# Conditioning weights fetched a step ahead into tiles of their own in the first layer of a three-block kernel

## The chip, the cores and the metric

The kernel runs on one core of one Trainium2 chip. The metric is the device time of one execution, in microseconds (us). One execution was also recorded by the hardware profiler; its rows are what the argument below is made from.

## What is computed

The input `x` is 1024 positions by 1024 channels in float32. Three blocks follow each other: a gated recurrent block (layer 0), a gated delta-rule block (layer 1) and a hybrid block of convolution and state space. Only layer 0 is touched by the change. Cut to what matters:

```python
c_act = silu(c)                                   # 1024 numbers
for i in range(2):
    cond = c_act @ ada_w[i] + ada_b[i]            # ada_w[i]: 1024 x 3072
    shift, scale, gate = cond[:1024], cond[1024:2048], cond[2048:]
    h = rmsnorm(x, norm_g[i]) * (1 + scale) + shift
    x = x + gate * block_i(h)

def block_0(h):                                   # rglru_block
    xb, zg = split(h @ in_w)                      # 1024 + 1024 columns
    xf = causal_dwconv(xb, conv_w) + conv_b       # 4 taps
    r, i = sigmoid(xf x gate_w[0..1] + gate_b)    # 8 blocks of 128 x 128
    a = exp(-8 * r * softplus(-lam))
    hseq = scan(a, sqrt(1 - a * a) * i * xf)      # along positions
    return (hseq * silu(zg)) @ out_w
```

`cond` has six parts, three for each layer: part 0 is the shift, 1 the scale, 2 the gate. Layer 0 needs its parts 1 and 0 before and during its input projection and its part 2 in its output projection. Parts 1 and 0 of layer 1 are needed by the norm that follows that output projection, part 2 of layer 1 only at the end of layer 1.

## The kernel before, in words

Channels lie on the 128 partitions and positions along the free dimension. A float32 matrix product is made as three float16 products of a high and a low half (`mm_chT`, L108 to L113; `mm_t`, L115 to L120). A weight set of 256 columns (`load_w`, L99) is fetched as one load of 1 MB into a staging tile `wst` (tag `st`, a ring of two), ScalarE makes the high half (L104), VectorE the low half (L105); that frees the staging tile. `wh` and `wl` are rings of four.

**Front (up to about 73 us).** `x` is loaded, normed and transposed in two halves of 512 positions. `ada_load` (L355) makes part 1 of layer 0, then part 0: for each it loads four blocks `sta` of 1 MB, sums 32 products on VectorE (`ada_acc`, L146 to L150, tile `accs`), turns the sums into columns by transposes on TensorE (L135) and a reduce (L368). `put_hT` (L376) writes the scaled halves `hTh` and `hTl`, and `lru_proj` (L297) projects the first pair of blocks. In the traced order part 0 (L410) stands ahead of the second half's `put_hT` (L414) and of its projection (L417).

**Recurrent stage (about 73 to 298 us).** Channels are taken as four pairs of blocks. `xbranch(p)` (L450) projects, convolves (`lru_conv`, L309), makes the gates (L482 to L485), and ends in the scan (L503) that writes `hs`. The gate tiles `gt0`, `gt1` have one buffer, so the gates of a pair wait for the scan of the pair before. `zbranch(p)` (L506) projects the other half, applies SiLU into `zs` (L515, a ring of three), multiplies by `hs` (L516) and writes high and low halves into a tile `y` (L517 through `split`, L122 to L125). `hs` and `y` share a ring of five (tag `a4`). Projections go through three banks `psmm`.

Between the branches stand nine calls of `ada_step` (L522). Each finishes the part taken up a step earlier (`ada_fin`, L162: four transposes, a reduce, an addition and a store) and takes up the next (`ada_part`, L152): two loads of 1 MB into the same `wst` ring that the weights use, followed at once by one multiplication (L148) and seven multiply-adds (L150) of 128x512 on VectorE. Eight half parts are made this way.

**Output projection (about 298 to 385 us).** For each of eight blocks of 128 positions, `out_proj` (L268) multiplies `y` by four weight sets, applies the gate (L276), adds `x` (L277), stores the result, and `norm_to_hT` (L242) makes the input of layer 1.

**What sets the order.** Engines run their instructions strictly in order. The framework fixes that order when the program is built: the order of the source is the priority, work under `tc.high_priority()` goes ahead, and what is ready by its own estimate of time is placed. All loads and stores of this part are issued by one queue, SyncE's (SP), also in order: an issue that waits for a tile holds those behind it.

## Time and profile before

| | us |
|---|---|
| median of 3 runs | 1914.98 |
| lowest, highest | 1912.77, 1927.49 |
| span of the profiled execution | 1914.6 |

The profile gives busy times of the engines: PE (TensorE matmuls), PEld (its weight loads, which overlap), DVE (VectorE), ACT (ScalarE), POOL (GpSimd), SP (SyncE). "PEclk" is the clock granted to TensorE as a share of full speed. A row of the timeline names start, duration, engine, line, operation, tiles and count; in brackets is how long the engine sat idle before it and what ended that. A wait is put down to the releaser that came last.

### The profile page before, as it was taken

The numbers are of one execution on the slowest core, as the hardware profiler recorded it, in microseconds if no ns is written. First come the engines' busy times: TensorE is split into PE (matmuls) and PEld (weight loads), VectorE is DVE, ScalarE is ACT, GpSimd is POOL, SyncE is SP. The second block draws the span as 40 slices with busy tenths as digits, with TensorE's granted clock in tenths as the row PEclk, the third lists the DMA queues.
The fourth block names the chain that finished last, engine by engine and source line by source line (L and its number), as shares of the span: only waits on it lengthen the run. The fifth ranks groups of instructions, "written<-read, shape, count | busy, mean of one in ns | idle before, by whom it ended". The sixth has DMA issues, their size and how long they took to land.

```text
span 1914.6 us, 29618 instructions
## 1 busy us (share of the span) xinstructions
PE 1808.0 (94%) x11847; PEld 1133.6 (59%) x11847; DVE 1450.2 (76%) x2472; ACT 935.7 (49%) x1673; POOL 52.8 (3%) x130
## 2 busy tenths in 40 slices
PE   5799789999899999999999999899999999999998
PEld 3344338855466656687878859556444444444487
DVE  6898876655786678877637689999999999594333
ACT  6567563356555666666434443465463121482221
POOL 0000001000000000001000020000000000000000
PEclk8899899999988899999889999999999999999999
DMA  9343255313131131224324322111221112102212
GB/s 336 108 154 85 93 154 188 105 52 84 31 88 39 27 102 30 79 78 138 91 93 155 115 37 71 38 51 53 92 75 54 57 56 77 45 23 66 78 67 89
DMA packets 161635, 165.26 MB, mean 86 GB/s; under 512 B 45662, under 2 KB 139934, under 8 KB 161498
## 3 DMA queue, kind: packets, MB, share of 16 engines
q1 hardware_dynamic: 161498, 163.38, 27.5%
q8 instruction: 93, 1.52, 0.3%
q14 instruction: 44, 0.36, 0.1%
HBM read 139.05 MB, written 23.12 MB: 85 GB/s over the span
## 4 chain that ended last, share of the span: by engine, by line
PE 51%; DVE 29%; ACT 7%; DMA 6%; issue 6%; SPq 1%; POOL 0%; DVEq 0%; ACTq 0%; POOLq 0%
DVE cc L990 5%; PE psmm L112 3%; PE psmm L111 3%; PE psmm L113 3%; DVE wl L105 2%; DMA wst_ada<-in_ada_w_dram 2%; PE ps_out L120 2%; PE ps_out L118 2%; PE ps_out L119 2%; DVE Tt L763 2%; DVE tm L761 2%; PE ps_fin L118 1%; PE ps_fin L120 1%; PE ps_fin L119 1%; PE ps_zc L113 1%
## 5 line engine op out<-in xcount | busy, mean ns | idle before, releaser
L111 PE MATMUL psmm<-hTh,wh 128*128 128x512 f16 x896 | 347.3, 389 | 19.9 <-ACT zs L515 16.7
L112 PE MATMUL psmm<-hTl,wh 128*128 128x512 f16 x896 | 347.6, 388 | 0.1
L113 PE MATMUL psmm<-hTh,wl 128*128 128x512 f16 x896 | 346.4, 387 | 0.0
L990 DVE SCALAR_TENSOR_TENSOR cc<-cu,cols,cc 128x1024 f32<-128x1024 f32 (+1 forms) x270 | 302.2, 1170 | 0.9
L112 PEld LDWEIGHTS <-wh 128*128 128x128 f16 x1568 | 155.0, 99 | 194.7 <-issue 29.5
L113 PEld LDWEIGHTS <-wl 128*128 128x128 f16 x1568 | 155.1, 99 | 179.3 <-issue 13.4
L111 PEld LDWEIGHTS <-wh 128*128 128x128 f16 x1568 | 155.1, 99 | 178.0 <-issue 12.0
L105 DVE SCALAR_TENSOR_TENSOR wl<-wst,wh 128x2048 f16<-128x2048 f32 (+2 forms) x71 | 154.3, 2177 | 57.8 <-ACT wh L104 57.6
L104 ACT ACTIVATE wh<-wst 128x2048 f16<-128x2048 f32 (+2 forms) x71 | 128.6, 1813 | 116.8 <-PE ps_gs L112 27.7
L763 DVE TENSOR_TENSOR Tt<-Tt,tm 128x248 f32<-128x248 f32 (+30 forms) x248 | 77.7, 313 | 4.5
L761 DVE TENSOR_TENSOR tm<-Lp,Tt 128x248 f32<-128x248 f32 (+30 forms) x248 | 76.9, 310 | 4.2
L118 PE MATMUL ps_z<-wh,hTh 128*128 128x256 f16 x256 | 72.1, 282 | 0.0
L119 PE MATMUL ps_z<-wh,hTl 128*128 128x256 f16 x256 | 72.0, 281 | 0.0
L120 PE MATMUL ps_z<-wl,hTh 128*128 128x256 f16 x256 | 71.9, 281 | 0.0
L120 PE MATMUL ps_out<-wl,y 128*128 128x256 f16 x256 | 69.8, 273 | 0.1
L118 PE MATMUL ps_fin<-wh,merged 128*128 128x256 f16 x256 | 69.8, 273 | 0.0
L119 PE MATMUL ps_fin<-wh,merged 128*128 128x256 f16 x256 | 69.8, 273 | 0.0
L120 PE MATMUL ps_fin<-wl,merged 128*128 128x256 f16 x256 | 69.8, 273 | 0.0
L118 PE MATMUL ps_out<-wh,y 128*128 128x256 f16 x256 | 69.7, 273 | 0.0
L119 PE MATMUL ps_out<-wh,y 128*128 128x256 f16 x256 | 69.7, 273 | 0.0
L123 ACT ACTIVATE hTh<-ps_ht 128x512 f16<-128x512 f32 x32 | 17.3, 594 | 83.2 <-PE ps_ht L252 83.2
L701 ACT ACTIVATE jk<-ps_tk 128x128 f32<-128x128 f32 x128 | 35.7, 279 | 39.7 <-PE ps_tk L697 36.7
(535 smaller groups left out, 4171.7 us busy)
## 6 DMA issues: line engine op xcount, KB each, us to landing
wst<-in_w_in_dram SPq DMA_DIRECT2D x24, 1024.0 KB
wst_ada<-in_ada_w_dram SPq DMA_DIRECT2D x16, 1024.0 KB
wst<-in_gdn_in_w_dram SPq DMA_DIRECT2D x16, 1024.0 KB
xt<-in_x_dram SPq DMA_DIRECT2D x16, 512.0 KB
wst<-in_lru_in_w_dram SPq DMA_DIRECT2D x8, 1024.0 KB
sta<-in_ada_w_dram SPq DMA_DIRECT2D x8, 1024.0 KB
x_d<-xt SPq DMA_DIRECT2D x16, 512.0 KB
wst<-in_lru_out_w_dram SPq DMA_DIRECT2D x4, 1024.0 KB
```

Of the source, the lines that this page charges most:

```text
L104: act.activation(hi, st, AF.Copy, scale=WS)
L105: dve.scalar_tensor_tensor(out=lo, in0=st, scalar=WS, in1=hi, op0=ALU.mult, op1=ALU.subtract)
L111: pe.matmul(ps, wh[:, k, c0:c0 + P], ah(k), start=(k == 0), stop=False)
L112: pe.matmul(ps, wh[:, k, c0:c0 + P], al(k), start=False, stop=False)
L113: pe.matmul(ps, wl[:, k, c0:c0 + P], ah(k), start=False, stop=(k == nk - 1))
L118: pe.matmul(ps, ah(k), wh[:, k, :], start=(k == 0), stop=False)
L119: pe.matmul(ps, al(k), wh[:, k, :], start=False, stop=False)
L120: pe.matmul(ps, ah(k), wl[:, k, :], start=False, stop=(k == nk - 1))
L701: act.activation(jk, pst[:, P * c:P * (c + 1)], AF.Square, accum_out=kq[:, n, 4 * b + c:4 * b + c + 1])
L761: dve.tensor_tensor(out=tv, in0=Lp[:, j, j + 1:].unsqueeze(1).to_broadcast([P, 8, n]), in1=Tt[:, :, j:j + 1].to_broadcast([P, 8, n]), op=A ...
L763: dve.tensor_tensor(out=Tt[:, :, j + 1:], in0=Tt[:, :, j + 1:], in1=tv, op=ALU.subtract)
L990: dve.scalar_tensor_tensor(out=acc, in0=cus[j][:, i + t0:i + t0 + n], scalar=col("cw", j, i), in1=acc, op0=ALU.mult, op1=ALU.add)
```

## The change

1. `ada_part` is split into `ada_fetch` and `ada_sum`. A half part is fetched into four tiles `ast` of 128x1024 (512 KB each, a ring of four of its own) by four loads. The first fetch stands ahead of the recurrent stage; each `ada_step` now finishes an older half part, sums the one fetched a step before, and fetches the next. The sum tile `ad` has one buffer instead of two.
2. Part 2 of layer 1 (two of the eight half parts) leaves the recurrent stage. It is made with the old `ada_part` inside the output projection, after its blocks 3 and 5 in the source, and finished after the loop. The stage keeps six half parts and seven `ada_step`s.
3. The four transposes of `ada_fin` get high priority.
4. `zbranch` writes its high and low halves over the part of `hs` that it has just multiplied; the `a4` ring goes from five to four. The `zs` ring goes from three to two.
5. `xp` (input of the convolution) is a ring of three for all pairs, where odd and even pairs had two each.
6. In the front the second half's `put_hT`, its projection and the column parameters are traced ahead of part 0, and the load of the weight set `wz[0]` behind it.

Everything else in the file differs by removed comments only. The instructions of the arithmetic are the same in number and shape.

```diff
+    def ada_fetch(pl, l, part, h):
+        tiles = []
+        for kk in range(4):
+            st = pl.tile([P, 2, 512], F32, tag="ast", name="ast", bufs=4)
+            sp.dma_start(st, ada_src(l, part, h, 2 * kk, 2))
+            tiles.append(st)
+        return tiles, l, part, h
+
+    def ada_sum(pl, tiles, l, part, h):
+        acc = pl.tile([P, 512], F32, tag="ad", name="ad")
+        for kk, st in enumerate(tiles):
+            for k in range(2):
+                ada_acc(acc, st[:, k, :], 2 * kk + k)
+        return acc, l, part, h
...
     def ada_fin(pl, acc, l, part, h):
-            pe.transpose(pst[:, P * kk:P * (kk + 1)], acc[:, P * kk:P * (kk + 1)], ident)
+            pe_ht(pst[:, P * kk:P * (kk + 1)], acc[:, P * kk:P * (kk + 1)], ident)
...
-        xp = (pl if p % 2 else gwp).tile([P, T + 3], F32, tag="xp", name="xp", bufs=2)
+        xp = gwp.tile([P, T + 3], F32, tag="xp", name="xp", bufs=3)
...
         load_x(1)
+        prows = load_cols(pl, PB, 7)
         wx.append(load_w(a["lru_in_w"][0], WC))
         norm_x(1)
-        wz.append(load_w(a["lru_in_w"][0], D))
+        for k in range(NK):
+            put_hT(xTp(1, k), k, 1)
+        for e in range(2):
+            lru_proj(xps[e], wx[0], e, 1)
+        with tc.high_priority():
+            set_cols(*prows)
         ada_load(0)
...
-        for k in range(NK):
-            put_hT(xTp(1, k), k, 1)
-        prows = load_cols(pl, PB, 7)
-        for e in range(2):
-            lru_proj(xps[e], wx[0], e, 1)
-        with tc.high_priority():
-            set_cols(*prows)
+        wz.append(load_w(a["lru_in_w"][0], D))
...
-                hs = ypool.tile(PR, F32, tag="a4", name="hs", bufs=5)
+                hs = ypool.tile(PR, F32, tag="a4", name="hs", bufs=4)
...
-                y = ypool.tile([P, 2, 2, T], F16, tag="a4", name="y", bufs=5)
...
-                        zs = pl.tile([P, 512], F32, tag="zs", name="zs", bufs=3)
+                        zs = pl.tile([P, 512], F32, tag="zs", name="zs", bufs=2)
...
-                        split(y[:, e, 0, HF[hf]], y[:, e, 1, HF[hf]], zs)
-            adq = [(l, part, h) for l, part in ((0, 2), (1, 1), (1, 0), (1, 2)) for h in range(2)]
-            adp = []
+                        y = hseq[p][:, e, HF[hf]].bitcast(F16)
+                        yT[-1].append((y[:, :512], y[:, 512:]))
+                        split(y[:, :512], y[:, 512:], zs)
+            adq = [(l, part, h) for l, part in ((0, 2), (1, 1), (1, 0)) for h in range(2)]
+            adt, adp = [ada_fetch(pl, *adq.pop(0))], []
...
                 if adp:
                     ada_fin(pl, *adp.pop(0))
+                if adt:
+                    adp.append(ada_sum(pl, *adt.pop(0)))
                 if adq:
-                    adp.append(ada_part(pl, *adq.pop(0)))
+                    adt.append(ada_fetch(pl, *adq.pop(0)))
...
                 if i > 0:
                     norm_to_hT(pl, i - 1, xo.pop(i - 1), G, SH)
+                if i in (3, 5):
+                    adp.append(ada_part(pl, 1, 2, len(adp)))
+            for q in adp:
+                ada_fin(pl, *q)
```

## Rows read from the trace of the kernel before

**Rows 1.** The page: span, busy time of two engines, and 40 slices of PE

```profile
span 1914.6 us, 29618 instructions
PE 1808.0 (94%) x11847; PEld 1133.6 (59%) x11847; DVE 1450.2 (76%) x2472; ACT 935.7 (49%) x1673; POOL 52.8 (3%) x130
...
PE   5799789999899999999999999899999999999998
```

**Rows 2.** Busy time by stretch: stretch, length, each engine's busy us, clock, DMA, GB/s

```profile
46.00:62.00 16.00, 7.00 (x38) 4.70 (x37) 15.80 (x37) 7.60 (x12) 0.00 (x0) 0.70 0.28 73
62.00:73.00 11.00, 11.00 (x57) 5.21 (x56) 6.19 (x20) 3.33 (x7) 0.14 (x2) 0.98 0.00 0
...
73.00:298.00 225.00, 195.56 (x1133) 94.80 (x1131) 185.87 (x224) 147.90 (x161) 5.51 (x9) 0.94 0.45 134
...
298.00:368.00 70.00, 70.00 (x644) 63.23 (x642) 46.66 (x79) 16.54 (x31) 1.54 (x2) 1.00 0.41 129
```

**Rows 3.** Chain of waits through 73 to 298 us: shares, then pieces (start, us, what)

```profile
by line: DMA wst_ada<-in_ada_w_dram 20.4%; DVE ad L150 11.1%; DMA wst<-in_lru_out_w_dram 6.5%; DVE xf L312 6.5%; DVE hs L503 5.9%; DMA wst<-in_lru_in_w_dram 5.0%; DVE wl L105 3.9%; ACT wh L104 3.4%; issue 3.2%; DVE gt L496 2.0%; DVE at L500
...
115.81 8.30 DMA wst_ada<-in_ada_w_dram
...
203.35 11.30 DMA wst_ada<-in_ada_w_dram
...
257.74 14.67 DMA wst<-in_lru_out_w_dram
```

**Rows 4.** The instructions on `wst_ada`: ns min/median/max, first and last start; idle until

```profile
L150 DVE SCALAR_TENSOR_TENSOR ad<-wst_ada,ccol,ad x56: 701/752/755, 92.7 to 257.0; 128x512 f32<-128x512 f32 x56
...
L148 DVE TENSOR_SCALAR ad<-wst_ada,ccol x8: 478/484/488, 90.8 to 247.1; 128x512 f32<-128x512 f32 x8
...
  DMA wst_ada<-in_ada_w_dram: 14.4, 5
```

**Rows 5.** Timeline of VectorE: the longest of the five waits, and the scan behind it

```profile
214.68 0.75 DVE L150 SCALAR_TENSOR_TENSOR ad<-wst_ada,ccol,ad 128x512 f32<-128x512 f32 x1 [5.60 <-DMA wst_ada<-in_ada_w_dram]
215.35 4.46 DVE L503 TENSOR_TENSOR_SCAN hs<-gt,at 128x1024 f32<-128x1024 f32 x2
```

**Rows 6.** PE's waits, 38 to 300 us: in total, times, longest

```profile
PE psmm L111 <- ACT zs L515: 16.7, 5, 7.4
PE ps_ada L135 <- DVE accs L150: 8.3, 3, 7.0
PE ps_ada L166 <- DVE ad L150: 5.4, 1, 5.4
```

**Rows 7.** The instructions on `ps_ada`: ns min/median/max, first and last start

```profile
L167 DVE TENSOR_REDUCE adac<-ps_ada x8: 682/686/692, 108.6 to 259.5; 128x4 f32<-128x512 f32 x8
...
L166 PE MATMUL ps_ada<-ident,ad x32: 272/273/448, 104.1 to 259.1; 128*128 128x128 f32 x32
```

**Rows 8.** Timeline of ScalarE: its longest wait for a weight load in the stage

```profile
272.43 1.91 ACT L104 ACTIVATE wh<-wst 128x2048 f16<-128x2048 f32 x1 [7.24 <-DMA wst<-in_lru_out_w_dram]
```

**Rows 9.** Timeline of TensorE: its longest wait in the stage

```profile
277.95 0.58 PE L111 MATMUL psmm<-hTh,wh 128*128 128x512 f16 x1 [7.38 <-ACT zs L515]
```

**Rows 10.** Timeline of VectorE in the front: sums of part 0

```profile
52.36 4.04 DVE L150 SCALAR_TENSOR_TENSOR accs<-sta,ccol,accs 128x256 f32<-128x256 f32 x10
```

**Rows 11.** Timeline of TensorE in the front: its longest wait there

```profile
56.15 0.66 PE L135 MATMUL ps_ada<-ident,accs 128*128 128x128 f32 x2 [6.99 <-DVE accs L150]
```

**Rows 12.** Chain of waits, 38 to 73 us: single matmuls of 128x512 at both clocks

```profile
62.07 0.43 PE psmm L112
...
64.08 0.22 PE psmm L111
```

**Rows 13.** Lines, 73 to 298 us: the convolution's multiply-adds; busy us, mean ns, idle before

```profile
L312 DVE SCALAR_TENSOR_TENSOR xf<-xp,cols,xf 128x1024 f32<-128x1024 f32 x24 | 30.7, 1282 | 0.8 <-ACT xf L310 0.6
```

**Rows 14.** Waits of SP's queue, 72 to 300 us: in total, times, longest

```profile
SPq L157 <- DVE ad L150: 39.3, 10, 12.5
...
SPq L101 <- DVE ad L150: 15.3, 4, 7.3
```

**Rows 15.** ScalarE's wait for input weights, 72 to 300 us: in total, times, longest

```profile
ACT wh L104 <- DMA wst<-in_lru_in_w_dram: 13.0, 4, 4.4
```

More of the change, by code (lines that the diff above doesn't have):

```diff
@@ L150, in ada_acc, with ada_src @@
             dve.scalar_tensor_tensor(out=acc, in0=st, scalar=ccol[:, k:k + 1], in1=acc, op0=ALU.mult, op1=ALU.add)
+    def ada_src(l, part, h, k0, n):
+        c0 = D * part + 512 * h
+        return a["ada_w"][l, P * k0:P * (k0 + n), c0:c0 + 512].rearrange("(k p) c -> p k c", p=P)
+    def ada_fetch(pl, l, part, h):
[11 more added lines that the diff above has]
+        return acc, l, part, h
     def ada_part(pl, l, part, h):
@@ L155, in ada_part @@
             st = wstage("wst_ada").rearrange("p (k c) -> p k c", k=4)
-            c0 = D * part + 512 * h
-            sp.dma_start(st, a["ada_w"][l, 4 * P * kk:4 * P * (kk + 1), c0:c0 + 512].rearrange("(k p) c -> p k c", p=P))
+            sp.dma_start(st, ada_src(l, part, h, 4 * kk, 4))
             for k in range(4):
@@ L506, in zbranch @@
             def zbranch(p, w):
-                y = ypool.tile([P, 2, 2, T], F16, tag="a4", name="y", bufs=5)
                 sb = shift_proj(w)
                 for e in range(2):
-                    yT.append(y[:, e])
+                    yT.append([])
                     for hf in range(2):
@@ L540 @@
             zbranch(1, wz[1])
-            ada_step()
             wz.append(load_w(a["lru_in_w"][0], D + 3 * WC))
@@ L544 @@
             xbranch(3, wx[3])
-            ada_step()
             ada_step()
@@ L559 @@
                 if i < NT:
-                    xo[i] = out_proj(ws, lambda k, i: yT[k][:, 0, P * i:P * (i + 1)],
-                                     lambda k, i: yT[k][:, 1, P * i:P * (i + 1)], pl, GA, i, x_in[TS[i], :])
+                    xo[i] = out_proj(ws, lambda k, i: yT[k][i // 4][0][:, TS[i % 4]],
+                                     lambda k, i: yT[k][i // 4][1][:, TS[i % 4]], pl, GA, i, x_in[TS[i], :])
                     sp.dma_start(x1_d[TS[i], :], xo[i])
```

## The prediction

> **What bounds the kernel now.** The page comes first: TensorE is busy for 94% of the span, and its lowest digits after the start lie in slices 2 and 4 to 7 of 40, which are layer 0 [rows 1]. The busy times by stretch then show three states of layer 0 [rows 2]. From 46 to 62 us VectorE is the limit (15.8 of 16 us) and TensorE works 7.0 us; in the next 11 us it is the other way round (VectorE 6.2, TensorE 11.0). From 73 to 298 us, the recurrent stage, none is full: TensorE 195.6 of 225, VectorE 185.9, ScalarE 147.9. From 298 to 368 us TensorE is full and VectorE two thirds busy.
>
> So the recurrent stage has room, and the chain of waits shows what holds it: loads of the conditioning weights are its largest item, 20.4% of 225 us, their sums the second with 11.1%, the loads of the output weights the third with 6.5% [rows 3]. That is not 46 us to be won. A load on the chain may have been issued late because something else was late, and with it gone the next slowest chain counts. The tile's own rows say what the engine lost: five waits of VectorE, 14.4 us in all [rows 4]. The longest, 5.6 us, stands directly before the scan of the third pair [rows 5], and the next pair's gates wait for that scan, so it moves everything behind it. TensorE's waits are the other side of the same stage: 16.7 us for `zs`, 5.4 us for a conditioning sum, inside the 225 - 195.6 = 29.4 us that it stood idle [rows 2, 6].
>
> **The change part by part.** The sum goes against the profiled execution, 1914.6 us; the median of the runs is 0.4 us higher, so I take a result of the sum for the median.
>
> *Fetch a step ahead.* A half part's load is issued one `ada_step` earlier, into tiles that the weights do not share. The stage has eight branches in 225 us, 28 us each. The two longest conditioning loads on the chain took 8.3 and 11.3 us [rows 3]. A load issued a branch ahead should have landed: the 14.4 us of waits go. Bounds: 0 (the wait moves to another operand) to 14.4.
>
> *The two half parts moved.* One costs VectorE 0.484 + 7 x 0.752 = 5.75 us [rows 4], a reduce of 0.69 us [rows 7], and an addition I leave out: 6.4 us, 12.9 for both. VectorE was busy for 185.9 of the 225 - 14.4 = 210.6 us in which no such wait held it, but the recurrence also passes through ScalarE and TensorE; I count about half, 6 us. Bounds 0 to 12.9.
>
> *The ring of staging tiles.* The first load of output weights started at 257.7 us, when the last sums (to 257.0 + 0.7) had freed a staging tile, and took 14.7 us [rows 3, 4]. ScalarE stood 7.24 us at the conversion behind it [rows 8], and the halves of `y` stood behind that, so `zs` stayed full and TensorE waited 7.38 us at 277.95 [rows 9]. After the change no conditioning sum holds a staging tile in this stage: 7.4 us, bounds 0 to 7.4.
>
> Together 14.4 + 6 + 7.4 = 27.8 us. These overlap: a scan that comes earlier meets the next limit. I take 0.7 of it, 19.5 us, because three engines that are each 65 to 87% busy do not give back all of a wait; bounds 0 and the removal of TensorE's whole idle time, 29.4 us, with part of what its low clock cost. The granted clock of the stage was 0.94 [rows 2]; with two levels of 1 and one half that is 12% of 225 = 27 us at the low one, half of it lost: 13.5 us.
>
> *Front.* VectorE worked off the ten multiply-adds of part 0 at 52.4 us [rows 10] while TensorE waited 7.0 us [rows 11] and the halves `hTl` were outstanding. With these first, the projection starts earlier and the sums run under it. VectorE remains the limit of the front, so its idle time in 62 to 73 us, 11.0 - 6.2 = 4.8 us, is the bound. I take 4; bounds 0 and 9 (TensorE's idle time in 46 to 62 us).
>
> *`zs` with two tiles.* One half product less can wait for its scan. A half is 24 matmuls of 0.22 us [rows 12], 5.2 us. Where the last scan is late, TensorE stops one half sooner and has that half left over: +5.2 us once. Bounds: 0 (the halves of `y` now come without the load in their way) to 15.6, three of four branches.
>
> *Part 2 of layer 1 in the output projection.* Eight transposes at 0.27 us, 2.2 us by their durations; they are pipelined and I count 1.2 us on TensorE, which is full there; bounds 0 and 2.2. The 12.9 us of VectorE lie under TensorE: 46.7 + 12.9 = 59.6 of 70 us [rows 2]. If that cover were gone, a load of 8 to 11 us would hold VectorE and, past the three banks, TensorE.
>
> *The rest at nothing.* `xp` with three tiles: hidden as long as three multiply-adds of 1.28 us [rows 13] end before the block after next is projected; at worst one such chain, 3.8 us, for three pairs, 11.5 us. `hs` written over: each half is read by the multiplication just before, so the only new waits are VectorE's and ScalarE's own order. The first fetch: TensorE's and VectorE's work of the front hides it, the DMA being idle from 62 to 73 us [rows 2].
>
> Sum: 1914.6 - 4 - 19.5 + 5.2 + 1.2 = 1897.5, which I give as 1897 us.
>
> **What the queue could do to it.** SP issues in order. Conditioning loads already waited there 39.3 us for sums, and weight loads 15.3 us for the same sums [rows 14]. After the change four fetches stand in that queue instead of two, each waiting for the sums of the half part before, and weight loads behind them wait too. ScalarE already stood 13.0 us, four times, for input weights [rows 15]. On this the Trainium skill, "DMA: Bandwidth & Descriptors", section "Anatomy of one DMA — SWDGE (gpsimd) path", says that any semaphore wait happens on the issuing sequencer before dispatch; by that rule, the rows agreeing, a blocked fetch delays every later load on SP.
>
> **The rivals.**
>
> *A. TensorE becomes the limit.* The waits were the whole of the recurrence's excess: TensorE's idle time falls from 29.4 to 5 us, 8 of the 13.5 us of low clock return, the front gives 4, the transposes take 1.2: 1914.6 - 24.4 - 8 - 4 + 1.2 = 1879 us. For it: the waits stand before the scans. Against: `zs` is shorter, and ScalarE is busy for 148 us with an order of its own.
>
> *B. The waits are replaced.* VectorE meets the next operand, `zs` costs its half once, and of the 27.8 us only about a third, 9.7, arrives, with 2 in the front: 1914.6 - 9.7 - 2 + 5.2 + 1.2 = 1909 us. For it: the sums themselves remain on the chain for six of eight half parts.
>
> *C. Weights late in SP's queue.* Each of five input weight loads waits for one more half part's sums, 5.75 us, in front of ScalarE: +29 us on the forecast, 1926 us; this decides once a load is late by over 3.5 us on average (17/5). Against: before, the shared ring made the same loads wait for the same sums.
>
> *D. A fetch does not fit into its step.* If a 512 KB load took as long as one of 1 MB and the four ran one after another, a half part would take 4 x 8.3 = 33 us, 5 more than the 28 us of a branch; six of them cost 30 us, and the 14.4 us would not be saved (0.7 x 14.4 = 10): 1897 + 30 + 10 = 1937 us. It decides from 7 us a load. Against: the DMA share in the stage is 0.45 [rows 2], and loads overlap. The Trainium skill, same page, section "Bandwidth", speaks for this side: it asks for loads of at least 1 MiB to reach 75% of peak, and the change halves them. By that section loads get less efficient; how much at this size no run here shows.
>
> **How the numbers follow.** Chances: the forecast (1888 to 1904) 0.44, A 0.20, B 0.25, C 0.07, D 0.04. A measurement of this kernel tells about 1% from no change, 19 us: below 1895.5 or above 1934. Faster by that: A and half of the forecast, 0.42; slower: D and little of C, 0.05; within 1%: 0.53. The range reaches from A's bound to above B and leaves out C and D and the best of A: 1874 to 1918.
>
> **What would show it.** Right: VectorE's idle time before L148 and L150 near zero in the stage; TensorE's wait for `zs` well under 16.7 us, with nothing like 7.4 us before the output projection; the stage's length, from the gates' weights to the first `ps_out`, near 205 us; TensorE full through the output projection. Wrong: ScalarE waiting for `wst` for more than 22 us in the stage (C); VectorE waiting for `ast` (D); TensorE's wait for `zs` as long as before (B); waits in the output projection behind `wst_ada`.

## The result and the profile after

The changed kernel takes 1930.2 us (median of 20 runs, 1924.1 to 1933.3) beside 1918.5 us for the kernel before (20 runs): a ratio of 1.0058 with the interval 1.0045 to 1.0071. So it is some 11 us slower, where 1897 us was forecast; 1930 lies above the range of 1874 to 1918, and the difference is under the 1% that the prediction called no change. The profiled execution of after spans 1926.9 us, that of before 1914.6 [rows 1].

The page of after, its span, busy times and the 40 slices of TensorE:

```profile
span 1926.9 us, 29657 instructions
...
PE 1814.7 (94%) x11847; PEld 1137.5 (59%) x11847; DVE 1447.6 (75%) x2472; ACT 937.0 (49%) x1674; POOL 51.2 (3%) x130
...
PE   5786998999899999999999999899999999999998
```

Against [rows 1] slice 4 falls from 9 to 6, slices 5 and 6 rise, slices 3 and 7 lose one, and the rest is the same. In before the low digits of layer 0 are those of slices 5 and 6 (7 and 8); the prediction's "slices 2 and 4 to 7" counts 4 and 7, which are 9, with them. The busy times by stretch say more (stretch, length, busy us of PE, PEld, DVE, ACT and POOL with their instructions, granted clock, DMA share, GB/s):

```profile
46.00:62.00 16.00, 15.91 (x90) 8.62 (x89) 8.52 (x11) 10.35 (x16) 0.00 (x0) 1.00 0.33 111
62.00:73.00 11.00, 10.36 (x50) 4.72 (x49) 11.00 (x29) 4.18 (x4) 0.00 (x0) 1.00 0.17 49
73.00:298.00 225.00, 188.16 (x1092) 91.50 (x1091) 180.78 (x227) 147.05 (x160) 5.50 (x11) 0.89 0.46 119
298.00:368.00 70.00, 63.78 (x566) 56.72 (x564) 51.45 (x93) 16.80 (x31) 0.00 (x0) 0.95 0.61 182
...
73.00:98.00 25.00, 15.19 (x118) 7.13 (x117) 25.00 (x64) 11.83 (x16) 0.20 (x2) 0.73 0.74 250
98.00:140.00 42.00, 39.25 (x233) 18.52 (x232) 41.48 (x53) 32.61 (x34) 0.20 (x2) 0.96 0.59 141
140.00:171.00 31.00, 11.98 (x73) 5.46 (x70) 24.81 (x26) 16.57 (x19) 0.00 (x0) 0.67 0.64 149
171.00:200.00 29.00, 26.94 (x118) 12.02 (x119) 21.55 (x26) 19.34 (x21) 0.10 (x1) 0.94 0.47 130
200.00:298.00 98.00, 94.79 (x556) 48.36 (x555) 67.94 (x63) 66.70 (x73) 5.00 (x6) 0.97 0.26 64
```

Against [rows 2] TensorE does in 46 to 62 us what it did later (15.9 us instead of 7.0), as meant. But it has two holes in the recurrent stage, 73 to 98 us (15.2 of 25) and 140 to 171 us (12.0 of 31), each at a granted clock of 0.73 and 0.67, means between the full level of 2.4 GHz and the half one of 1.2, to which the clock falls behind the waits; between and behind them it is nearly full. And in the output projection, where before it was full for 70 of 70 us, it stands for 6.2 us.

The item in the change's title did its work. The chain of waits through 73 to 298 us, the four-tile ring's own rows and TensorE's waits from 38 to 300 us (in total, times, longest):

```profile
by line: PE psmm L112 9.3%; PE psmm L111 9.3%; PE psmm L113 9.1%; issue 6.9%; DVE xf L331 6.1%; DMA ast<-in_ada_w_dram 5.9%; DVE wl L105 4.9%; DVE ad L150 4.8%; DVE hs L522 3.9%; ACT L533 2.3%; ACT gt L504 2.2%; DVE at L518 2.0%; DVE at L51
...
139.15 13.31 DMA ast<-in_ada_w_dram
```

```profile
L150 DVE SCALAR_TENSOR_TENSOR ad<-ast,ccol,ad x42: 741/752/753, 88.8 to 234.7; 128x512 f32<-128x512 f32 x42
...
  DMA ast<-in_ada_w_dram: 4.7, 1
```

```profile
PE psmm L111 <- ACT zs L533: 15.8, 2, 13.6
PE ps_gate L501 <- ACT xh L123: 7.9, 4, 4.7
PE ps_ada L135 <- DVE ad L150: 6.1, 2, 3.9
```

The conditioning loads fall from 20.4 to 5.9% of the chain [rows 3] and VectorE's waits for them from 14.4 us in five to 4.7 us in one [rows 4]. The one that is left belongs to a load issued at 139.15 us that took 13.3 us, and it stands in the second hole: VectorE stands 4.7 us, ScalarE behind it, and TensorE 13.6 us at `zs`. Why that load took so long is taken up at the end of "Which link of that chain".

To see where time is won and lost in the kernels below, three points are read from their timelines: the first matmul of the output projection (`ps_out`), the last transposes of its norm (`ps_ht`) and the store of the next layer's decays (`gb_d`), in us from the start. The ratios are those of the timed runs, each kernel beside its own runs of the kernel before. From the third point on before and after issue the same instructions in the same order. Each row is one execution: in after, a_own, a_wab, a_plainm and a_noload, whose source differs only behind the stage, `ps_out` lies between 285.5 and 288.8 us, so that a difference of some 3 us between two rows tells nothing by itself.

| kernel | ratio to before, interval | `ps_out` | `ps_ht` | `gb_d` | `ps_out` to `gb_d` |
|---|---|---|---|---|---|
| before | 1 | 289.8 | 385.2 | 409.4 | 119.6 |
| after | 1.0058 (1.0045 to 1.0071) | 288.6 | 393.3 | 417.6 | 129.0 |
| b_moved | 1.0041 (1.0025 to 1.0058) | 288.3 | 384.8 | 416.1 | 127.8 |
| a_kept | 0.9988 (0.9975 to 1.0000) | 285.2 | 380.5 | 403.8 | 118.6 |
| a_own | 1.0070 (1.0049 to 1.0092) | 288.8 | 394.8 | 419.7 | 130.9 |
| a_front | 0.9976 (0.9958 to 0.9995) | 276.2 | 380.9 | 405.4 | 129.2 |
| a_wab | 0.9998 (0.9977 to 1.0018) | 285.5 | 386.5 | 411.0 | 125.5 |
| a_plainm | 1.0014 (0.9993 to 1.0035) | 286.3 | 383.3 | 414.6 | 128.3 |
| a_noload | 0.9974 (0.9953 to 0.9996) | 287.1 | 385.3 | 409.2 | 122.1 |
| b_front | 1.0041 (1.0028 to 1.0054) | 300.5 | 396.0 | 420.5 | 120.0 |
| a_wz | 0.9940 (0.9921 to 0.9960) | 271.7 | 377.1 | 401.2 | 129.5 |
| b_zs2 | 1.0002 (0.9991 to 1.0013) | 295.6 | 390.9 | 414.2 | 118.6 |
| a_front_kept | 0.9928 (0.9903 to 0.9953) | 278.8 | 374.8 | 398.5 | 119.7 |
| a_wz_kept | 0.9903 (0.9886 to 0.9921) | 277.4 | 372.7 | 396.0 | 118.6 |

The last column is the cleanest: 118.6 to 120.0 us in every kernel without the moved part, 122.1 to 130.9 in every kernel with it. 129.0 - 119.6 = 9.4 us are lost there. `ps_out` itself hardly moved (289.8 to 288.6), so what the stage gained was lost in the stage or ahead of it. As `ps_out` comes before 298 us, the row of 73 to 298 us holds the first 8 to 9 us of the output projection too.

### The profile page after: what moved, and what is told of

It is laid out like the page before. It is cut to its first block, busy times and chain, and to the rows that moved or that the text cites. A ratio compares the mean times of both kernels' runs of the same rounds, so it can differ in the third digit from the quotient of the medians.

```text
span 1926.9 us, 29657 instructions
## 1 busy us (share of the span) xinstructions
PE 1814.7 (94%) x11847; PEld 1137.5 (59%) x11847; DVE 1447.6 (75%) x2472; ACT 937.0 (49%) x1674; POOL 51.2 (3%) x130
## 4 chain that ended last, share of the span: by engine, by line
PE 53%; DVE 29%; ACT 7%; issue 6%; DMA 3%; SPq 1%; POOL 0%; DVEq 0%; ACTq 0%; POOLq 0%
DVE cc L1016 5%; PE psmm L112 4%; PE psmm L113 4%; PE psmm L111 4%; DVE wl L105 2%; PE ps_out L120 2%; PE ps_out L118 2%; PE ps_out L119 2%; DVE Tt L789 2%; DVE tm L787 2%; PE ps_fin L120 1%; PE ps_fin L118 1%; PE ps_fin L119 1%; PE ps_zc L112 1%; PE ps_zc L111 1%
## 5 line engine op out<-in xcount | busy, mean ns | idle before, releaser
L111 PE MATMUL psmm<-hTh,wh 128*128 128x512 f16 x896 | 348.2, 389 | 18.3 <-ACT zs L533 15.8
L111 PEld LDWEIGHTS <-wh 128*128 128x128 f16 x1568 | 155.4, 99 | 178.6 <-issue 13.6
L120 PE MATMUL ps_out<-wl,hs 128*128 128x256 f16 x256 | 70.4, 275 | 0.0
L118 PE MATMUL ps_out<-wh,hs 128*128 128x256 f16 x256 | 70.4, 275 | 0.0
L119 PE MATMUL ps_out<-wh,hs 128*128 128x256 f16 x256 | 70.3, 275 | 0.0
L727 ACT ACTIVATE jk<-ps_tk 128x128 f32<-128x128 f32 x128 | 35.7, 279 | 39.9 <-PE ps_tk L723 36.8
```

What stands on the lines that cost most here:

```text
L111: pe.matmul(ps, wh[:, k, c0:c0 + P], ah(k), start=(k == 0), stop=False)
L118: pe.matmul(ps, ah(k), wh[:, k, :], start=(k == 0), stop=False)
L119: pe.matmul(ps, al(k), wh[:, k, :], start=False, stop=False)
L120: pe.matmul(ps, ah(k), wl[:, k, :], start=False, stop=(k == nk - 1))
L727: act.activation(jk, pst[:, P * c:P * (c + 1)], AF.Square, accum_out=kq[:, n, 4 * b + c:4 * b + c + 1])
```

## The experiments

### One part alone, one part undone

*b_moved* is the kernel before with nothing but part (1,2) moved to the output projection, in the old routine with the shared staging tiles.

```
-adq = [(l, part, h) for l, part in ((0, 2), (1, 1), (1, 0), (1, 2)) for h in range(2)]
+adq = [(l, part, h) for l, part in ((0, 2), (1, 1), (1, 0)) for h in range(2)]
...
-ada_step()
...
-ada_step()
...
+    if i in (3, 5):
+        adp.append(ada_part(pl, 1, 2, len(adp)))
+for q in adp:
+    ada_fin(pl, *q)
```

> The kernel before with the moved part alone: part 2 of layer 1 leaves the recurrent stage and is made in the output projection by the old routine, through the staging ring that the weights share; all else as before. From the first ps_out matmul to the last ps_ht transposes the kernel before took 95.5 us, the changed one 104.7. Theory 1 (the ring: the small weight load for the decay columns of layer 1 now queues behind the sums, and ScalarE, in order, stands at its conversion): this stretch becomes 103 to 107 us here too, the recurrent stage gains 0 to 6 us, and the whole is 1918 to 1927 beside about 1918.5 before. Rival (the loss in the output projection comes from the new places of the state or from tiles of the stage before): the stretch stays at 95 to 97 us and the whole is 1912 to 1919.

*a_kept* is the changed kernel with that same piece undone: the part stays in the recurrent stage, with eight half parts in nine steps.

> The changed kernel with part 2 of layer 1 kept in the recurrent stage, fetched and summed there like the other six half parts, in nine steps. Theory 1: the output projection is back at 95 to 97 us (9 us less than the changed kernel), the stage pays 0 to 13 us for two more sums: 1917 to 1932, most likely 1924. Rival: the stretch stays at 103 us or more although nothing is made there, and the whole is over 1930.

*a_own* leaves the part in the output projection and gives it the fetched tiles of its own there:

```
+    if i == 1: adt.append(ada_fetch(pl, 1, 2, 0))
+    if i == 3: adp.append(ada_sum(pl, *adt.pop(0))); adt.append(ada_fetch(pl, 1, 2, 1))
+    if i == 5: ada_fin(pl, *adp.pop(0)); adp.append(ada_sum(pl, *adt.pop(0)))
```

> The changed kernel, with the moved part fetched into four tiles of its own in the output projection too, so that the staging ring holds only weights there; sums and transposes as many as in the changed kernel. Theory 1 (the shared ring is the cause of the output projection's loss): the stretch from first ps_out to last ps_ht is 96 to 99 us and the whole 1920 to 1924. Rival (the added work on VectorE and the transposes are the cause, wherever their data lie): 102 to 106 us, the whole 1927 to 1932.

*a_front* is the changed kernel with the front of before: z weights' load and part 0's sums ahead of the second half's projection, parameter rows behind them.

> The changed kernel with the order of the kernel before in the front (part 0 ahead of the second half's projection, the weight set wz[0] ahead of part 0). Theory 2 (the new order costs: the shift halves shl come 17 us later, the gate weights' second load waits, and TensorE stands idle between 73 and 98 us): shl is ready near 67 us, the first scan ends 3 to 8 us earlier than the 134.5 us of the changed kernel, and the whole is 1922 to 1927. Rival (the early projection of the second half pays for it): the whole is 1930 to 1938.

Measured: b_moved 1927.3 us (1.0041), a_kept 1918.0 (0.9988), a_own 1934.5 (1.0070), a_front 1914.1 (0.9976). Two parts of the change cost time, each by itself. The moved part costs 1.0058 - 0.9988 = 0.0070, 13 us, in the changed kernel, and 0.0041, 8 us, alone in the kernel before. The new front costs 1.0058 - 0.9976 = 0.0082, 16 us. a_own lets the shared staging ring fall as the moved part's whole price: with tiles of its own the last column is 130.9 us, no less than with shared ones. Not all came as expected: in b_moved `ps_out` to `ps_ht` is 96.5 us and not theory 1's 103 to 107, though the whole is as slow as theory 1 said; a_own takes longer than even its rival's 1927 to 1932 us; and a_front gains more than its 1922 to 1927 us.

The trace of after shows how the moved part gets at TensorE. SyncE's queue in 290 to 325 us, then ScalarE, VectorE and TensorE (start, length, idle before and what ended it):

```profile
295.12 0.38 SPq L176 DMA_DIRECT2D wst_ada<-in_ada_w_dram  x1
...
317.52 0.38 SPq L176 DMA_DIRECT2D wst_ada<-in_ada_w_dram  x1
...
323.11 0.38 SPq L101 DMA_DIRECT2D wst<-in_gdn_in_w_dram  x1
...
330.15 0.31 ACT L104 ACTIVATE wh<-wst 128x128 f16<-128x128 f32 x1 [5.80 <-DMA wst<-in_gdn_in_w_dram]
...
331.53 0.15 DVE L256 TENSOR_SCALAR lnss<-lnss 128x1 f32<-128x1 f32 x1 [4.61 <-ACT hn L252]
...
332.60 0.75 DVE L150 SCALAR_TENSOR_TENSOR ad<-wst_ada,ccol,ad 128x512 f32<-128x512 f32 x1
...
333.40 1.12 PE L135 MATMUL ps_ada<-ident,ad 128*128 128x128 f32 x4 [5.26 <-DVE ad L150]
```

Four loads of the part (two of them shown), the last at 317.52, stand ahead of the next layer's first weight load, the small one of 16 columns, which goes out at 323.11 us. In the kernel before it went out at 296.43:

```profile
296.43 0.38 SPq L101 DMA_DIRECT2D wst<-in_gdn_in_w_dram  x1
```

ScalarE has that conversion next in its order and stands 5.8 us; VectorE's norm waits for ScalarE; the part's last sums wait in VectorE's order; its transposes wait for the sums, and TensorE, where they are high in the order, waits 5.3 us for them; over 320 to 340 us, with that wait in it, its granted clock is 0.83, where before it was 1.00. In a_own the load went out at 318.80 us, behind the fetches, and ScalarE stood longer still:

```profile
318.80 1.36 SPq L101 DMA_DIRECT2D wst<-in_gdn_in_w_dram  x2
...
329.07 0.31 ACT L104 ACTIVATE wh<-wst 128x128 f16<-128x128 f32 x1 [14.96 <-DMA wst<-in_gdn_in_w_dram]
```

In b_moved, whose transposes are at plain priority, TensorE is full through the loop, and the price is paid behind it, where the next layer's first matmuls stand, for which the profile names no releaser:

```profile
PE ps_ab L119 <- issue: 4.1, 1, 4.1
```

### Which link of that chain

*a_wab* takes the first link out: the small load and its conversion stand ahead of the loop.

```
+wab = load_w(a["gdn_in_w"][0], 4 * D, ncols=16)
 GA = bcast_row(pl, ada_d[0, 2 * D:3 * D], "GA")
...
-wab = load_w(in_w, 4 * D, ncols=16)
```

> The changed kernel with one load moved: the 16 columns of gdn_in_w (64 KB) for the next layer's decay and beta are loaded and converted ahead of the output projection's loop, so in front of the moved part's four 1 MB loads instead of behind them. Theory W (the late small load is the cause: ScalarE stands 5.8 us at its conversion, VectorE behind it, the moved part's last sums behind that, TensorE at their transposes): the wait of TensorE for ad (6.2 us) falls below 1.5 us, the stretch from 104.7 to 96 to 99 us, the time to 1921 to 1925. Theory T (the transposes stand too early in TensorE's queue, whatever holds the sums): TensorE still waits 4 us or more for ad and the time stays within 3 us of the changed kernel. A third case, in which the next wide load of gdn_in_w takes the small one's place: ScalarE waits at that one, stretch 101 to 104 us.

*a_plainm* takes the last one out: in the loop's final lines `ada_fin` transposes at plain priority.

> The changed kernel with the eight transposes of the moved part alone at the priority that they had before, which puts them behind all of the output projection's matmuls instead of among them; ScalarE's order is the same. Theory T (the early transposes hold TensorE): no wait of TensorE for ad inside the loop, stretch 95 to 98 us to the last norm transposes, but the next layer's first weights and the store of the rows come later, so that some 2 to 6 us of it may come back at the loop's end; time 1918 to 1925. Theory W (ScalarE's and VectorE's stall holds TensorE by itself, through the three banks of the output projection): TensorE waits 4 us or more for freed banks in place of ad and the time stays at 1928 to 1932.

*a_noload* takes the loads out; its sums read another row.

```
-adp.append(ada_part(pl, 1, 2, len(adp)))
+acc = pl.tile([P, 512], F32, tag="ad", name="ad", bufs=2)
+for k in range(8):
+    ada_acc(acc, GA[:, 512 * (k % 2):512 * (k % 2) + 512], k)
+adp.append((acc, 1, 2, len(adp)))
```

> The changed kernel with the moved part's four 1 MB loads left out: its 16 sums take the gate row that lies in SBUF, so their values are not part (1,2)'s; sums, transposes, reductions and stores stay. Theory L (the loads are the cause, by standing ahead of the next layer's weights): the small load of gdn_in_w is issued before 300 us, no wait of TensorE for ad above 1.5 us, gb_d store 119 to 122 us behind the first output-projection matmul (after: 129.0), time 1918 to 1922. Theory E (the part's own engine work is the cause: 16 sums of 0.75 us on VectorE and 8 transposes of 0.27 us on TensorE): 125 us or more, time within 3 us of the changed kernel.

TensorE's waits from 270 to 420 us in a_wab, and ScalarE's longest:

```profile
PE ps_ada L135 <- DVE ad L150: 2.4, 2, 1.7
...
335.13 1.91 ACT L104 ACTIVATE wh<-wst 128x2048 f16<-128x2048 f32 x1 [9.93 <-DMA wst<-in_gdn_in_w_dram]
```

The wait for `ad` falls from 6.2 to 2.4 us, `ps_out` to `ps_ht` from 104.7 to 101.0, the last column from 129.0 to 125.5 and the ratio from 1.0058 to 0.9998: theory W's direction, short of its bounds, and with it the third case that was named: the next, wide load of the same weights now holds ScalarE 9.9 us. In a_plainm no wait for `ad` is left and the norm's last transposes come 97.1 us after `ps_out` instead of 104.7, but 7 us of this come back behind the loop (128.3 in the last column), where TensorE stands as in b_moved:

```profile
PE ps_ab L119 <- issue: 4.5, 1, 4.5
```

So theory T names a place where the loss shows, not its cause: with the transposes out of the way it shows elsewhere. a_noload decides. Its small load goes out three microseconds ahead of before's place, and the wait for `ad` nearly ends:

```profile
293.59 0.38 SPq L101 DMA_DIRECT2D wst<-in_gdn_in_w_dram  x1
...
PE ps_ada L135 <- DVE ad L150: 1.6, 2, 1.0
```

The last column is 122.1 us and the time 1920.1. Of the 9.4 us the loads make 129.0 - 122.1 = 6.9; the sums, transposes and reductions by themselves 122.1 - 119.6 = 2.5 us, which is about the 2.2 us of eight transposes [rows 7]. Theory L holds: no wait for `ad` is over its 1.5 us, and its 122 us are missed by 0.1. By the timed ratios a_wab, a_plainm and a_noload gain more on after (0.0060, 0.0044 and 0.0084, or 12, 8 and 16 us) than by the last column (3.5, 0.7 and 6.9 us). After was timed beside other runs of the kernel before than these three, and where the rest was gained is not shown.

One thing in this chain is not the late issue. In after the small load goes out at 323.11 us, before ScalarE comes free for it at 324.35, and is used 7.0 us after its issue. Ahead of it in the queue stands a store of the moved part itself, `ada_d`, 2 KB that go out as 512 single numbers of four bytes; the high-priority transposes bring it into the loop. In a_plainm the same small load, with no such store ahead of it yet, is used 2.3 us after its issue, and ScalarE stands 2.2 us instead of 5.8. The store of after, then the load and its use in a_plainm:

```profile
321.58 0.38 SPq L189 DMA_DIRECT2D ada_d<-adac  x1
...
320.27 0.38 SPq L101 DMA_DIRECT2D wst<-in_gdn_in_w_dram  x1
...
322.59 0.31 ACT L104 ACTIVATE wh<-wst 128x128 f16<-128x128 f32 x1 [2.20 <-DMA wst<-in_gdn_in_w_dram]
```

In a_own the store goes out 0.4 us ahead of the small load, which is used 10.3 us after its issue; so a_own does not tell what the queue alone costs. The same shows in the recurrent stage. Take the 13.3 us load of after, which goes out with three more fetches and behind a load of output weights: the store ahead of it, and two 8 us stretches behind that:

```profile
135.89 0.37 SPq L189 DMA_DIRECT2D ada_d<-adac  x1
...
139.00:147.00 8.00, 4.10 (x19) 2.11 (x18) 6.75 (x8) 7.97 (x11) 0.00 (x0) 0.94 0.30 36
147.00:155.00 8.00, 1.15 (x33) 0.93 (x32) 3.14 (x3) 0.65 (x3) 0.00 (x0) 0.50 0.99 357
```

and in before, where the store goes out at 200.49 us and the load that took 11.3 us [rows 3] at 203.35:

```profile
203.00:209.00 6.00, 5.27 (x26) 2.28 (x24) 5.53 (x5) 3.52 (x5) 0.00 (x0) 1.00 0.13 23
209.00:214.00 5.00, 5.00 (x25) 2.27 (x24) 0.08 (x1) 3.32 (x5) 0.00 (x0) 1.00 0.68 202
```

Over the fourteen traces, 65 of these stores up to 345 us have a weight load issued within 4 us behind them: from 5 to 9 us after the store the DMA moves 36 GB/s (the median; over 100 in six), from 12 to 14 us after it 310. Behind 103 weight loads of the same stretch with no such store in the 16 us ahead it moves 359 GB/s from 2 to 4 us after the issue (the median). So the long loads of the stage, before and after, follow the conditioning's own stores. No run takes the stores away or moves them alone: that they are the cause is likely and not shown, and what they cost is open.

### The front

*b_front* is the kernel before with the new front order alone. *a_wz* is the changed kernel with one step of it moved back, the first z weights' load and conversion:

```
 norm_x(1)
+wz.append(load_w(a["lru_in_w"][0], D))
 for k in range(NK):
     put_hT(xTp(1, k), k, 1)
...
-wz.append(load_w(a["lru_in_w"][0], D))
 for e in range(2):
     lru_conv(xf0[:, e], xps[e], e)
```

> The kernel before with only the front's new order (parameter rows early, second half's hT and projection ahead of part 0's sums, first z weights last). The prediction gave the order 4 us of gain. Theory G (the order costs by itself, since the gate weights' second load stands behind the z weights' in SyncE's queue): slower by 8 to 16 us, 1.004 to 1.008, first output-projection matmul at 298 us or later. Theory I (it costs only together with the four tiles' fetch, which is issued behind the gate weights and so came 13 us late): within 4 us of the kernel before or faster, and first matmul at 284 to 292 us.

> The changed kernel with one step of its front moved back: the load and conversion of the first z weights stand ahead of the second half's hT and projection again, while part 0's sums stay behind them. Theory G (the second load of the gate weights stands in SyncE's queue behind the z weights' staging tile, and ScalarE stands 15.6 us at its conversion): the gate weights are issued before 70 us, ScalarE's wait falls below 6 us, the first output-projection matmul comes 6 to 12 us earlier (277 to 283), time 1918 to 1924. Theory S (part 0's sums, 61 to 80 us, are what is late: shl at 84 us instead of 67): shl stays at 80 us or later, and the time stays within 4 us of the changed kernel.

Measured: b_front 1932.1 us, 1.0041, with `ps_out` at 300.5 us, so the order costs some 8 us by itself (theory G; theory I falls). a_wz 1912.7 us, 0.9940, with `ps_out` at 271.7, 17 us earlier than in after and more than theory G said (6 to 12); the shift columns of part 0 (`shl`) still come at 82.5 us, so theory S falls. The rows of after: VectorE's half of the z weights' conversion, SyncE's queue, and ScalarE at the gate weights:

```profile
75.60 2.28 DVE L105 SCALAR_TENSOR_TENSOR wl<-wst,wh 128x2048 f16<-128x2048 f32 x1
...
61.16 0.37 SPq L453 DMA_DIRECT2D gst<-in_lru_gate_w_dram  x1
...
77.90 0.37 SPq L453 DMA_DIRECT2D gst<-in_lru_gate_w_dram  x1
...
78.95 2.92 SPq L161 DMA_DIRECT2D ast<-in_ada_w_dram  x4
...
81.83 1.06 ACT L123 ACTIVATE gwh<-gst 128x1024 f16<-128x1024 f32 x1 [15.61 <-DMA gst<-in_lru_gate_w_dram]
```

and the same in a_wz:

```profile
60.66 2.28 DVE L105 SCALAR_TENSOR_TENSOR wl<-wst,wh 128x2048 f16<-128x2048 f32 x1
...
59.57 3.76 SPq L453 DMA_DIRECT2D gst<-in_lru_gate_w_dram  x2
...
65.28 5.55 SPq L161 DMA_DIRECT2D ast<-in_ada_w_dram  x4
...
66.87 1.06 ACT L123 ACTIVATE gwh<-gst 128x1024 f16<-128x1024 f32 x1 [2.60 <-DMA gst<-in_lru_gate_w_dram]
```

The gate weights are staged in the same two tiles as the other weights, and the second of their loads takes the tile after the z weights. With the z weights last in the front, VectorE turns to them behind part 0's sums, at 75.60 us; the tile is free at 77.88, the load goes out at 77.90 (the profile names as its releaser a reduction that VectorE runs next, at 77.80). In a_wz these are 60.66, 62.94 and some 63 us. ScalarE stands 15.6 us for it in after and 2.6 in a_wz, and the first fetch of the new ring, behind it in SyncE's queue, goes out 13.7 us later. On this the Trainium skill, "DMA: Bandwidth & Descriptors", section "Anatomy of one DMA — SWDGE (gpsimd) path", says that any semaphore wait happens on the issuing sequencer before dispatch; here, on SyncE's queue, the trace agrees: a load that waits for its tile holds four fetches with free tiles, which go out 13.7 us later than in a_wz. The second hole shrinks with it. Busy times of a_wz, and of a_front in the first stretch:

```profile
73.00:98.00 25.00, 15.24 (x114) 6.97 (x112) 24.86 (x71) 11.65 (x16) 0.20 (x2) 0.73 0.56 189
...
140.00:171.00 31.00, 22.26 (x150) 10.58 (x149) 26.69 (x28) 19.28 (x23) 0.00 (x0) 0.89 0.64 164
...
73.00:98.00 25.00, 24.86 (x172) 12.01 (x171) 24.36 (x52) 19.66 (x25) 0.23 (x2) 1.00 0.61 191
```

The first hole stays in a_wz (15.2 us of 25) and is gone in a_front (24.9), where part 0's sums stand ahead of the projection again: it belongs to these late sums, which the change put there and a_wz leaves there. In the second TensorE works 22.3 us instead of 12.0, and its wait for `zs` is 0.5 us from 73 to 298 us, where after has 15.8.

### The ring of `zs`, and both losses undone

*b_zs2* is the kernel before with two `zs` tiles instead of three.

> The kernel before with the ring of zs tiles cut from three to two and nothing else. The prediction priced it at 5.2 us in the changed kernel: ratio about 1.003. Rival, TensorE waits at other tiles anyway: within 0.001 of 1. Rival, its ring paces the z branches: 1.006 or more.

1926.6 us against 1925.7, 1.0002 with the interval 0.9991 to 1.0013: between 1.7 us won and 2.5 lost, so the timed runs put the 5.2 us that the prediction set for it out, in the kernel before. Its one profiled execution does not agree: `ps_out` comes 5.8 us and `gb_d` 4.8 us later than in before's, whose execution is the fastest of the fourteen behind `gb_d` (1505.2 us). The timed runs decide on the whole; a small cost in the stage is not excluded. In the changed kernel the ring was not tried alone.

*a_front_kept* undoes the front's order and the moved part; *a_wz_kept* undoes the z weights' place and the moved part, and keeps the sums behind the projection.

> The changed kernel with two of its parts undone together: the front in the order of the kernel before, and part (1,2) kept in the recurrent stage (8 half parts, 9 steps). The four fetched tiles, the fetch a step ahead and the output in place of the state stay. If front and moved part cost their shares independently, the gains add: 1930.2 - 16.1 (front order alone) - 12.2 (part kept alone) = 1902, about 0.991 to 0.994 of the kernel before; first output-projection matmul at 273 to 277 us, output-projection stretch (first matmul to last transposes) 95 to 97 us. Rival: both undo the same TensorE wait further on, or the kept part fills the stage again by what the front gives back: then 1910 to 1916, and the first output-projection matmul stands at 282 us or later.

> The changed kernel with two steps undone: the first z weights' load stands ahead of the second half's projection again, and part (1,2) is kept in the recurrent stage. All else of the change stays, part 0's sums behind the projection too. If both losses are as a_wz and a_kept show them and add: 0.9988 + 0.9940 - 1.0058 = 0.987 of the kernel before, some 1895 to 1899; first output-projection matmul at 268 to 274 us, next layer's gb_d store 119 us behind it (before 119.6, after 129.0). Rival: the kept part's two loads and eight sums refill the stage that a_wz freed, first matmul at 278 us or later, ratio 0.992 or more, as a_front_kept gave (0.9928).

Measured: 1909.7 us, 0.9928, and 1907.0 us, 0.9903 (0.9886 to 0.9921). The first is as expected in its ratio (0.991 to 0.994; the 1902 us stood against a kernel before at 1918.5, which took 1923.7 beside this one), with `ps_out` 1.8 us past the range; the second stands between both readings, since the kept part does refill the stage a little: `ps_out` at 277.4 us, where a_wz had 271.7. It is the fastest kernel here, 19 us (0.0097 x 1925.7) below the kernel before, and these are its stretches:

```profile
73.00:298.00 225.00, 200.24 (x1198) 101.94 (x1197) 197.71 (x265) 149.97 (x165) 5.18 (x11) 0.92 0.54 137
298.00:368.00 70.00, 70.00 (x641) 63.15 (x639) 49.40 (x74) 20.73 (x35) 1.24 (x2) 1.00 0.39 125
```

TensorE works 200.2 us of the first stretch instead of 188.2 (20.6 us of it are output projection, where after has 9.4) and is full again in the output projection. From 73 us to `ps_out` it takes 204.4 us instead of 215.6.

## Why the prediction was wrong

The account, in ratios to before: what a_front_kept holds (fetch a step ahead into own tiles, output in place of the state, shorter rings) is worth 0.9928 - 1 = -0.0072, 14 us; the moved part adds 0.9976 - 0.9928 = 0.0048, 9 us; the front's order adds 1.0058 - 0.9976 = 0.0082, 16 us. Together -14 + 9 + 16 = +11 us. The prediction had -14.3 (19.5 won, 5.2 lost), +1.2 and -4. The first term was right in size, and the two small ones decided the sign. The shares depend on the order in which the parts are undone: by a_kept first, the moved part is 0.0070 and the front 0.9988 - 0.9928 = 0.0060, 13 and 12 us. The sign of each is the same in both orders.

*Fetch a step ahead and the staging ring:* right in kind and, as a sum, in size. VectorE's waits fell from 14.4 to 4.7 us, the output weights' wait of 7.2 us [rows 8] and TensorE's 7.4 us [rows 9] are gone, and 14 us arrived (by the interval 9 to 19), against 0.7 x (14.4 + 7.4) = 15.3 by the prediction's terms without the moved sums, or 10.1 with the loss at `zs`. The whole stage agrees: a_front, with six half parts and the old front, takes 276.2 - 73 = 203.2 us from 73 us to `ps_out`, before 216.8, 13.6 less, where the terms of the stage gave 19.5 - 5.2 = 14.3 and the prediction looked for a stage near 205. The share of 0.7 was a guess that held, and in part by luck: the single terms were not tried apart, nor was the fetch a step ahead put into the kernel before alone. One reading under them was wrong. The load at 257.74 us is the second of the output weights, not the first:

```profile
249.96 8.15 SPq L101 DMA_DIRECT2D wst<-in_lru_out_w_dram  x2
```

and its 14.7 us count from its issue, when it had its staging tile: an `ada_d` store goes out at 263.45 us, and from 263 to 270 us the DMA moves 79 GB/s. Likewise the prediction took 8.3 and 11.3 us for what a load of 1 MB takes; these follow such stores too.

*`zs` with two tiles:* the step was too dear. It priced a half of 5.2 us for TensorE, and by the timed runs of b_zs2 it costs at most 2.5 us in the kernel before. In a_wz, with the z weights early, the waits at `zs` are 0.5 us.

*The moved sums:* 0.7 x 6 = 4.2 us were booked as a gain of the stage. Where the stage is undisturbed, `ps_out` comes 277.4 - 271.7 = 5.7 us (a_wz_kept to a_wz) or 278.8 - 276.2 = 2.6 us (a_front_kept to a_front) earlier without them: about the size, from single executions. But the same part costs 9 us in the output projection.

*Part 2 in the output projection, 1.2 us:* the failed step. The prediction counted the transposes and laid VectorE's 12.9 us under TensorE's full time. The engine work cost 2.5 us, over the 1.2 and just over the bound of 2.2. It left out the part's four loads of 1 MB. The prediction's own paragraph on SyncE's queue says that a blocked issue delays every later load, but it was applied to the fetches of the stage alone; these four were moved in front of the next layer's weights in that queue and in the two staging tiles. Nor did the prediction give a term to the high priority of the transposes, which brings the part's stores and TensorE's wait for `ad` into the loop: with plain priority (a_plainm) the ratio is 1.0014 instead of 1.0058, though the last column falls by 0.7 us only. The sentence on a lost cover ("would hold VectorE and, past the three banks, TensorE") named the right victims, but looked for the part's own load, not for the one behind it.

*Front, -4 us:* the failed step that cost most. That the projection starts earlier and the sums run under it did happen (TensorE 15.9 of 16 us from 46 to 62 us, against 7.0 [rows 2]). With the z weights left where they were it is worth something: a_wz against a_front 0.0036, a_wz_kept against a_front_kept 0.0025, some 5 to 7 us, though the intervals overlap, so that a gain of about the forecast's 4 is likely and not shown. What was not costed is the other half of the same edit, the z weights' conversion put behind part 0's 14 us of sums, in an order where the gate weights wait for its staging tile and the first fetches wait for the gate weights. Undoing that half alone gives 1.0058 - 0.9940 = 0.0118, 23 us (a_wz), more than the whole front costs. The prediction followed the staging ring in the stage and not in the front.

*The rivals.* C comes nearest: a weight load late in SyncE's queue in front of ScalarE, at 1926 us, "against: before, the shared ring made the same loads wait for the same sums". It looked for input weights behind the new fetches in the stage; the late loads were the gate weights ahead of the stage and the next layer's weights behind it. B (the waits are replaced) fits the profile's look, with TensorE's wait for `zs` as long as before (15.8 against 16.7 us [rows 6]), yet in a_wz, with the z weights early, it is 0.5 us. D fell: six half parts of four loads kept up with their steps but for one load of 13.3 us, which follows a store as the slow 1 MB loads of before do. A did not come: TensorE's idle time in the stage rose from 29.4 to 36.8 us. Two of the signs of being wrong that the prediction listed came: the long wait for `zs`, and waits in the output projection for weights that were issued behind `wst_ada`.

## What to carry to other kernels

A step that is moved takes its loads along: for each, list what stands behind it in the issuing queue and in its staging ring, over the next stage too, and ask which in-order engine has the late tile next. It takes its stores along as well: here a 2 KB store in single numbers was followed by some 10 us of slow loads. A weight's staging tile is free only when the last engine that reads it gets there, so putting a conversion behind a long run of sums delays the loads after the next, not only its own matmuls. And where a change bundles several moves, cost the small ones as carefully: here the large gain came about as forecast, and two edits booked at a few microseconds turned the sign.

## What the runs showed of the hardware

The granted clock differs between executions in stretches where the order of instructions and the busy time are the same. From 20 us of the next layer's work, in before and at the same point of after (8.3 us later):

```profile
720.00:740.00 20.00, 20.00 (x134) 13.93 (x132) 17.48 (x40) 14.51 (x40) 0.10 (x1) 0.97 0.12 27
```

```profile
728.30:748.30 20.00, 20.00 (x124) 14.04 (x124) 16.39 (x34) 13.35 (x34) 0.10 (x1) 0.88 0.11 27
```

TensorE is busy throughout in both and does 134 and 124 matmuls. Its clock is 0.97 and 0.88: with a full level of 2.4 GHz and a half one of 1.2, that is 6 and 24% of the 20 us at the half level. In the 20 us ahead it was busy for 18.6 us in both, at 0.95 and 0.87. From the `gb_d` store to the end the profiled execution of before takes 1914.6 - 409.4 = 1505.2 us, that of after 1926.9 - 417.6 = 1509.3, that of a_kept 1918.3 - 403.8 = 1514.5, with the same instructions in the same order; the other eleven lie between. So some 4 to 9 us of a difference between two single profiles can be clock alone, and the verdicts above go by the timed ratios, with the profiles telling only where. What sets the clock apart in such stretches was not tried.
